# A trunk kernel whose S5 mixer changes between token order and chunk order: 64 ScalarE copies replaced by round trips through DRAM

## The chip, the cores and the metric

The kernel runs on one core of one Trainium2 chip. TensorE (PE; its weight loads are listed as PEld) multiplies, VectorE (DVE) and ScalarE (ACT) work elementwise, GpSimd (POOL) does a little arithmetic and issues some DMAs, and the sync engine (SP) issues the loads of the weights. The metric is the device time of one execution in microseconds (us), lower is better.

## The reference

A decoder trunk of two layers works on 256 tokens of width 1024. Each layer is a SwiGLU block, a token mixer, a second SwiGLU block (each followed by a layer norm) and a gate on an embedding. The mixer of the first layer has two halves, SSD and S5, on one input projection. Only S5 is touched:

```python
def s5_mixer(u, lam_re, ..., d_skip, w_glu, b_glu):      # u: (1, 256, 1024)
    ug = u.reshape(b, l, 64, 16)                          # 64 groups of 16 channels
    bu = jnp.einsum('blgp,gnp->blgn', ug, b_bar)          # complex states
    _, states = lax.associative_scan(linear_recurrence_combine, (a, bu), axis=1)
    y = jnp.real(jnp.einsum('blgn,gpn->blgp', states, c)) + d_skip * ug
    y = jax.nn.gelu(y.reshape(b, l, 1024))
    y = y * jax.nn.sigmoid(y @ w_glu + b_glu)
    return y
```

## The kernel before, in words

Weights come from DRAM in units of 1 MB (`wst`, two buffers, issued by SP). ACT casts each unit to a high part `wh` (line 61), DVE subtracts to get the low part `wl` (line 62), and every product is made of three matmuls. The kernel is one straight program for all engines; each engine works off its own instructions in order. That order is not written by hand: a scheduler sets it from estimated durations when the program is built, so a change of instructions also moves others.

The S5 mixer cuts the 256 tokens into 64 chunks of 4 steps. Its inputs u come as 1024 channels in two halves c = 0, 1 of 512. For each half, the projection is evicted from PSUM into `uT`, a tile of 128 channel partitions by 4 channel blocks by 256 tokens (lines 643 and 645; one of the two evictions of a half is on ACT, the other on DVE). In `U` a partition holds one step and one channel of a group of 32, and the free dimension holds 32 blocks of 64 chunks. So 32 partitions of `uT` with every fourth token go to another set of 32 partitions of `U`. Before, ACT does this by 16 copies of 32 partitions by 4 x 64 elements for each half (line 657). They read every fourth element.

The recurrence runs in 8 batches (`s5_batch`, called as recur(0) to recur(7)), of which 0 to 3 use the first half of U and 4 to 7 the second. A batch is a product with U on PE (`s5v`, line 678), a chain of rotation, scan and rotation on DVE (lines 686 to 694, result `S`), and a product back on PE (`s5y`, line 701), copied by ACT into `G` (line 703). Between the batches stand the projections of the SSD half (`bc`, `xs`, `z`). After four batches ACT applies the Gelu to `G` in place (line 709), and 16 ACT copies bring G back to channel partitions and token order in `yT` (line 719); they write every fourth element. `yT` is split into `yh` (ACT, line 722) and `yl` (DVE, line 723), the operands of the gate's product `glu` (lines 741 to 743). Tanh of it (`th`) times yT (line 746) is split again into `s5h` and `s5l` and goes to the output projection.

Batches are independent of the SSD half, whose heads (`seg`, `E`, `yp`, `cp`) run mostly behind the last batch.

Of the kernel before, what the change touches and what calls it, by code (L numbers as in the profile page):

```python
# [8 lines left out]
F32 = mybir.dt.float32  # L9
# [3 lines left out]
ALU = mybir.AluOpType  # L13
# [4 lines left out]
P = 128  # L18
D = 1024
NTOK = 256  # L20
# [13 lines left out]
def f32(ap):  # L34
    return ap.bitcast(F32)
# [49 lines left out]
def late(g, ins):  # L85

    g.tc.keep_in_program_order(ins)
# [10 lines left out]
def new_xT(g, name):  # L98
    return [g.xt.tile([P, KT, NTOK], F32R, tag=f"x{p}", name=f"x{p}_{name}") for p in "hl"]
# [532 lines left out]
    return e  # L632


def s5_inputs(g, pool, U, c):

    nc = g.nc
    uT = g.lnp.tile([P, 4, NTOK], F32, tag="ln_r", name=f"uT_{c}")

    def keep(h, ps):  # L640
        k = slice(2 * h, 2 * h + 2)
        if h:
            nc.vector.tensor_copy(uT[:, k, :], ps)
        else:
            nc.scalar.copy(uT[:, k, :], ps)

    if c:
        project_channels(g, f"u{c}", keep)
    else:
        channel_tiles(g, pool, f"u{c}", keep)  # L650
    Uv = U[:, 16 * c:16 * c + 16, :].rearrange("p (k q) c -> p k q c", q=4)
    uv = uT.rearrange("p k (c s) -> p k c s", s=4)
    for s in range(4):
        for q in range(4):
            dst = Uv[32 * s:32 * s + 32, :, q, :]
            src = uv[32 * q:32 * q + 32, :, :, s]
            nc.scalar.copy(dst, src)  # L657


def s5_batch(g, pool, U, G, b):  # L660
# [45 lines left out]
def s5_half_out(g, G, c, yh, yl):  # L706

    nc = g.nc
    op = nc.scalar.activation(G, G, AF.Gelu_apprx_tanh)
    if c:  # L710
        late(g, op)
    Gv = G.rearrange("p (k q) c -> p k q c", q=4)
    yT = g.lnp.tile([P, 4, NTOK], F32, tag="ln_r", name=f"yT_{c}")
    yv = yT.rearrange("p k (c s) -> p k c s", s=4)
    for q in range(4):
        for s in range(4):
            dst = yv[32 * q:32 * q + 32, :, :, s]
            src = Gv[32 * s:32 * s + 32, :, q, :]
            nc.scalar.copy(dst, src)  # L719
    for k in (0, 2):  # L720
        s, src = slice(4 * c + k, 4 * c + k + 2), yT[:, k:k + 2]
        nc.scalar.copy(yh[:, s], src)
        nc.vector.tensor_tensor(yl[:, s], src, f32(yh[:, s]), op=ALU.subtract)
    return yT


def s5_outputs(g, pool, yT, yh, yl):

    nc = g.nc
    hb = pool.tile([P, KT], F32, tag="hb", name="hb", bufs=1)  # L730
    nc.scalar.mul(hb, g.cols("bglu"), 0.5)
    sh = pool.tile([P, KT, NTOK], F32R, tag="sh", name="s5h", bufs=1)
    sl = pool.tile([P, KT, NTOK], F32R, tag="sl", name="s5l", bufs=1)
    for u in range(4):
        pieces = g.w.unit()
        for j in range(2):
            ct = 2 * u + j
            wh, wl = (p.rearrange("p (k c) -> p k c", k=KT) for p in pieces[j])
            ps = g.ps.tile([P, NTOK], F32, tag="acc", name=f"glu_{ct}", bufs=4)
            for k in range(KT):  # L740
                nc.tensor.matmul(ps, wh[:, k, :], yh[:, k, :], start=k == 0, stop=False)
                nc.tensor.matmul(ps, wh[:, k, :], yl[:, k, :], start=False, stop=False)
                nc.tensor.matmul(ps, wl[:, k, :], yh[:, k, :], start=False, stop=k == KT - 1)
            th = pool.tile([P, NTOK], F32, tag="th", name=f"th_{ct}", bufs=2)
            nc.scalar.activation(th, ps, AF.Tanh, scale=0.5, bias=hb[:, ct:ct + 1])
            nc.vector.scalar_tensor_tensor(th, th, 1.0, yT[ct // 4][:, ct % 4, :], op0=ALU.add, op1=ALU.mult)
            nc.scalar.mul(sh[:, ct, :], th, 0.5)
            nc.vector.scalar_tensor_tensor(sl[:, ct, :], th, 0.5, f32(sh[:, ct, :]), op0=ALU.mult, op1=ALU.subtract)
    return sh, sl


# [200 lines left out]
def ab_inputs(g, pool, s5pool, yh, yl):  # L952
# [37 lines left out]
    for c in range(2):  # L990
        s5_inputs(g, pool, U, c)
# [31 lines left out]
def channel_tiles(g, pool, name, out):  # L1023

    nc = g.nc
    ps = project(g, name, True)
    xb = []
    for t in range(NT):
        x = pool.tile([P, 512], F32, tag="ev", name=f"ev_{name}_{t}", bufs=2)
        nc.scalar.copy(x, ps[t])  # L1030
        xb.append(x)
    for h in range(2):
        tp = g.ps.tile([P, 2, NTOK], F32, tag="tr", name=f"ct_{name}_{h}", bufs=2)
        to_channels(g, xb, (2 * h, 2 * h + 1), tp)
        out(h, tp)
# [241 lines left out]
@with_exitstack  # L1277
def tile_trunk(ctx: ExitStack, tc: tile.TileContext, xnat, xTd, pT, lnr, colsd, cstd, abrow, abdt, s5bc, cdlr, cdgu,
               wall, out):
    nc = tc.nc  # L1280
    g = Ctx()
    g.nc, g.tc = nc, tc
    g.abrow, g.abdt, g.s5bc, g.cdlr, g.cdgu = abrow, abdt, s5bc, cdlr, cdgu
    g.const = ctx.enter_context(tc.tile_pool(name="const", bufs=1))
    g.wst = ctx.enter_context(tc.tile_pool(name="wst", bufs=2))
    g.wsp = ctx.enter_context(tc.tile_pool(name="wsp", bufs=6))
    g.xp = ctx.enter_context(tc.tile_pool(name="xp", bufs=1))
    g.xt = ctx.enter_context(tc.tile_pool(name="xt", bufs=1))
    g.lnp = ctx.enter_context(tc.tile_pool(name="lnp", bufs=2))
    g.small = ctx.enter_context(tc.tile_pool(name="small", bufs=2))  # L1290
    g.rows = ctx.enter_context(tc.tile_pool(name="rows", bufs=1))
    g.ps = ctx.enter_context(tc.tile_pool(name="ps", bufs=2, space=PSUM))
    g.dram = ctx.enter_context(tc.tile_pool(name="dram", bufs=1, space=DRAM))
    g.w = Weights(g, wall)
    g.lnr = lnr
    g.grow = {}

    nc.scalar.preload_act_table_set("silu_and_others")
    g.mhalf = g.const.tile([P, 1], F32, tag="mhalf", name="mhalf")
    nc.vector.memset(g.mhalf, -0.5)  # L1300
    g.s5dram = [g.dram.tile([P, PACK], F32, tag=f"s5d{b}", name=f"s5d{b}") for b in range(NB)]
    g.xT = new_xT(g, "in")
    for t in range(NT):
        xs = g.lnp.tile([P, KT, P], F32, tag="ln_r", name=f"xin_{t}")
        for h in range(2):
            s = slice(4 * h, 4 * h + 4)
            nc.scalar.dma_start(xs[:, s], xTd[t][:, s])
            split_xT(g, t, h, xs[:, s], g.xT)

    def load_constants():  # L1310
        cs = g.const.tile([P, cstd.shape[1]], F32, tag="cst", name="cs")
        nc.scalar.dma_start(cs, cstd)
        g.cst = lookup(cs, CST)
        g.ident = g.cst("ident")
        lc = g.const.tile([P, colsd.shape[1]], F32, tag="cols", name="lc")
        nc.scalar.dma_start(lc, colsd)
        g.cols = lookup(lc, COLS)

    def load_x():
        g.x = []  # L1320
        for t in range(NT):
            x = g.xp.tile([P, D], F32, tag=f"x{t}", name=f"x_in_{t}")
            late(g, nc.sync.dma_start(x, xnat[t * P:(t + 1) * P, :]))
            g.x.append(x)
        load_rows(g, 0, lnr)

    with tc.tile_pool(name="s5p", bufs=1) as s5p, tc.tile_pool(name="s5c", bufs=1) as s5c:
        g.s5p, g.s5c = s5p, s5c
        rest, half, loaded = [], [], []

        def first():
            load_constants()
            loaded.append(s5_load(g, 0))
            g.s5pe = s5c.tile([P, PACK_PE], F32, tag="s5pe", name="s5pe")
            nc.gpsimd.memset(g.s5pe[:, 1024:1536], 0.0)

        def params(b):
            if rest:
                rest.pop()()
            if b < NB:  # L1340
                if b % 4 == 0:
                    half[:] = [s5_half(g, b // 4, loaded[b // 4])]
                rest.append(s5_params(g, b, half[0]))
            if b == 3:
                loaded.append(s5_load(g, 1))

        hooks = {-1: first, 0: lambda: s5_scalars(g), NB + 2: load_x}
        for b in range(NB + 1):
            hooks[b + 1] = lambda b=b: params(b)
        ffn(g, "f00", 0, hooks)  # L1350
    mixer_ab(g, 1)
    load_rows(g, 2, lnr)
    with tc.tile_pool(name="pp0", bufs=1) as g.pp:
        ffn(g, "f01", 2)
        ple(g, 0, ple_proj(g, 0, pT), None)
    load_rows(g, 3, lnr)
    ffn(g, "f10", 3)
    load_rows(g, 4, lnr)
    mixer_cd(g, 4)
    load_rows(g, 5, lnr)  # L1360
    with tc.tile_pool(name="pp1", bufs=1) as g.pp:
        ffn(g, "f11", 5)
        ple(g, 1, ple_proj(g, 1, pT), out)
# [147 lines left out]
```

## Time and profile before

| | |
|---|---|
| time, median of 3 runs | 1270.6 us (1265.54, 1270.6, 1272.09) |
| the profiled execution's own time | 1264.66 us |
| its span | 1262.9 us |
| PE busy in it | 1210.2 us (96%) |
| DVE busy | 847.6 us (67%) |
| ACT busy | 660.9 us (52%) |
| POOL busy | 33.4 us (3%) |
| mean DMA rate | 188 GB/s |

The S5 mixer lies between about 225 and 445 us of the span. [...] A timeline row gives the start and the length of a run of equal instructions. "Idle" of PE costs time here; idle of the other engines does so only if PE waits for them.

### The profile page before, as it was taken

Reading aid. Unit: us, or ns where it says so; the run is one execution under the profiler, and the core shown is the slowest. Engines: PE = TensorE matmul, PEld = TensorE weight load, DVE = VectorE, ACT = ScalarE, POOL = GpSimd, SP = SyncE. Lnnn points to the kernel's source line nnn. Section 1 sums busy time; section 2 is a strip of 40 time slices with the busy share of each in tenths; the row PEclk is TensorE's granted clock in tenths of the full one; section 3 lists DMA queues with packets and bytes.
Section 4 is the critical chain, followed back from the end, with each engine's and each line's share of the span. In section 5 each row is a group of like instructions: output and inputs, shape, how many; then the busy total and the mean of one; then the engine's idle time right before and its main releaser. Section 6 shows DMA issues by size and latency. Waiting matters only on the chain.

```text
span 1262.9 us, 16242 instructions
## 1 busy us (share of the span) xinstructions
PE 1210.2 (96%) x6274; PEld 1020.0 (81%) x6274; DVE 847.6 (67%) x1353; ACT 660.9 (52%) x1008; POOL 33.4 (3%) x58
## 2 busy tenths in 40 slices
PE   6999999979896999999999999999999989999998
PEld 5888788779795987888888788888788877888886
DVE  6998774749685957645557655545779877555566
ACT  6566674584836653544444544444466635444434
POOL 0000000000000000000000000000100010000000
PEclk9999999989898999999999999999999999999999
DMA  7577767737551365655563655556443236555542
GB/s 272 202 250 249 264 249 280 265 128 256 179 193 41 119 208 172 211 199 178 189 224 110 233 191 180 196 184 215 157 164 134 100 109 218 196 187 200 173 160 100
DMA packets 39453, 237.93 MB, mean 188 GB/s; under 512 B 4528, under 2 KB 5200, under 8 KB 15696
## 3 DMA queue, kind: packets, MB, share of 16 engines
q1 hardware_dynamic: 30672, 206.06, 47.3%
q10 hardware_dynamic: 6096, 16.16, 3.8%
q0 software_dynamic: 2608, 14.68, 3.1%
q8 instruction: 49, 0.80, 0.3%
q14 instruction: 28, 0.23, 0.1%
HBM read 222.20 MB, written 14.68 MB: 188 GB/s over the span
## 4 chain that ended last, share of the span: by engine, by line
PE 86%; ACT 6%; DMA 3%; DVE 3%; issue 1%; ACTq 0%; POOL 0%; SPq 0%; DVEq 0%
PE gu_f L72 12%; PE gu_f L71 12%; PE gu_f L70 12%; PE acc_f L72 6%; PE acc_f L70 6%; PE acc_f L71 6%; DMA wst<-in_wall_dram 3%; ACT yT L719 2%; PE ht_f L209 1%; ACT U L657 1%; PE acc_ab L70 1%; PE acc_ab L71 1%; PE acc_ab L72 1%; DVE wl L62 1%; PE s5k L551 1%
## 5 line engine op out<-in xcount | busy, mean ns | idle before, releaser
L62 DVE TENSOR_TENSOR wl<-wst,wh 128x1024 fp32r<-128x1024 f32 (+1 forms) x378 | 453.4, 1215 | 281.0 <-ACT wh L61 275.0
L61 ACT CAST wh<-wst 128x1024 fp32r<-128x1024 f32 (+1 forms) x378 | 386.5, 1045 | 315.0 <-PE gu_f L72 104.1
L70 PE MATMUL acc_f<-wh,hh_f 128*128 128x512 f32 x352 | 137.5, 391 | 1.2 <-ACT hh_f L212 1.2
L71 PE MATMUL acc_f<-wl,hh_f 128*128 128x512 f32 x352 | 137.7, 391 | 0.0
L72 PE MATMUL acc_f<-wh,hl_f 128*128 128x512 f32 x352 | 136.4, 392 | 0.2 <-DVE hl_f L213 0.2
L70 PEld LDWEIGHTS acc_f<-wh,hh_f 128*128 128x128 f32 x352 | 66.1, 188 | 15.3 <-ACT hh_f L212 1.9
L72 PEld LDWEIGHTS acc_f<-wh,hl_f 128*128 128x128 f32 x352 | 66.1, 188 | 14.1 <-DVE hl_f L213 0.7
L71 PEld LDWEIGHTS acc_f<-wl,hh_f 128*128 128x128 f32 x352 | 66.1, 188 | 13.5
L70 PE MATMUL gu_f<-wh,xh_in 128*128 128x512 f32 x176 | 70.8, 407 | 6.1 <-ACT wh L61 6.1
L205 ACT ACTIVATE sg_f<-gu_f 128x256 f32<-128x256 f32 x88 | 33.6, 383 | 74.9 <-PE gu_f L72 73.1
L70 PE MATMUL gu_f<-wh,xh_ple 128*128 128x512 f32 x176 | 69.8, 396 | 1.8 <-ACT xh_ple L112 1.8
L71 PE MATMUL gu_f<-wl,xh_in 128*128 128x512 f32 x176 | 70.8, 404 | 0.0
L72 PE MATMUL gu_f<-wh,xl_in 128*128 128x512 f32 x176 | 70.6, 401 | 0.0
L70 PE MATMUL gu_f<-wh,xh_ab 128*128 128x512 f32 x176 | 69.8, 396 | 0.5 <-ACT xh_ab L112 0.5
L70 PE MATMUL gu_f<-wh,xh_cd 128*128 128x512 f32 x176 | 69.8, 396 | 0.3 <-ACT xh_cd L112 0.2
L72 PE MATMUL gu_f<-wh,xl_cd 128*128 128x512 f32 x176 | 69.1, 393 | 0.7 <-DVE xl_cd L113 0.7
L72 PE MATMUL gu_f<-wh,xl_ab 128*128 128x512 f32 x176 | 69.0, 392 | 0.7 <-DVE xl_ab L113 0.7
L71 PE MATMUL gu_f<-wl,xh_ab 128*128 128x512 f32 x176 | 68.8, 391 | 0.2 <-DVE wl L62 0.2
L72 PE MATMUL gu_f<-wh,xl_ple 128*128 128x512 f32 x176 | 68.8, 392 | 0.0
L71 PE MATMUL gu_f<-wl,xh_cd 128*128 128x512 f32 x176 | 68.7, 390 | 0.0
L71 PE MATMUL gu_f<-wl,xh_ple 128*128 128x512 f32 x176 | 68.7, 390 | 0.0
L206 DVE TENSOR_TENSOR sg_f<-sg_f,gu_f 128x256 f32<-128x256 f32 x88 | 36.5, 415 | 26.6 <-ACT sg_f L205 26.5
(467 smaller groups left out, 2443.1 us busy)
## 6 DMA issues: line engine op xcount, KB each, us to landing
wst<-in_wall_dram SPq DMA_DIRECT2D x185, 1024.0 KB, 4.9
s5d<-s5pk POOLq DMA_DIRECT2D x8, 896.0 KB, 4.8
s5d<-s5pe POOLq DMA_DIRECT2D x8, 768.0 KB, 3.7
row<-in_lnr_dram SPq DMA_DIRECT2D x12, 512.0 KB, 6.7
W<-s5d ACTq DMA_DIRECT2D x8, 512.0 KB, 3.9
Q<-s5d ACTq DMA_DIRECT2D x8, 512.0 KB, 5.8
tab<-s5d ACTq DMA_DIRECT2D x8, 384.0 KB, 3.8
wst<-in_wall_dram SPq DMA_DIRECT2D x4, 512.0 KB, 6.2
```

The lines of the kernel that those rows point to most:

```text
L61: ops = [nc.scalar.copy(wh[:, c], src[:, c])]
L62: ops.append(nc.vector.tensor_tensor(wl[:, c], src[:, c], f32(wh[:, c]), op=ALU.subtract))
L70: nc.tensor.matmul(out, xh, wh, start=first, stop=False)
L71: nc.tensor.matmul(out, xh, wl, start=False, stop=False)
L72: nc.tensor.matmul(out, xl, wh, start=False, stop=last)
L205: nc.scalar.activation(sg, ps[t][:, 0:256], AF.Silu)
L206: nc.vector.tensor_tensor(sg, sg, ps[t][:, 256:512], op=ALU.mult)
L209: nc.tensor.transpose(tp[:, k, :], sg[:, k * P:(k + 1) * P], g.ident)
L551: nc.tensor.matmul(kp[:, q, :], Eb[:, i, q, :], cv[:, i, hs.start + q, :], start=i == 0, stop=i == 1)
L657: nc.scalar.copy(dst, src)
L719: nc.scalar.copy(dst, src)
```

## The change

`uT` is now written step by step (all 64 chunks of step 0, then of step 1, and so on), so the evictions on lines 643 and 645 of before read their PSUM source with a stride of four elements. One DMA, issued by POOL, writes uT to a DRAM tile of 512 rows; four DMAs on the same queue, one for each step, read it back into 32 partitions of U each, in runs of 64 elements (256 bytes), 512 runs each. The outputs go the same way: one DMA writes G to DRAM, four read it into 32 partitions of yT each, again 512 runs of 256 bytes. yT, yh, yl, the gate's product and th now stand in step order. The product of line 746 reads th and yT in token order (every element 256 bytes from the last) and writes a new tile `gt` in token order, from which s5h and s5l are made.

```diff
+def by_step(ap):
+    return ap.rearrange("p k (s c) -> p k s c", s=4)
...
         if h:
-            nc.vector.tensor_copy(uT[:, k, :], ps)
+            nc.vector.tensor_copy(by_step(uT[:, k, :]), ps.rearrange("p k (c s) -> p k s c", s=4))
         else:
-            nc.scalar.copy(uT[:, k, :], ps)
+            nc.scalar.copy(by_step(uT[:, k, :]), ps.rearrange("p k (c s) -> p k s c", s=4))
...
-    Uv = U[:, 16 * c:16 * c + 16, :].rearrange("p (k q) c -> p k q c", q=4)
-    uv = uT.rearrange("p k (c s) -> p k c s", s=4)
-    for s in range(4):
-        for q in range(4):
-            dst = Uv[32 * s:32 * s + 32, :, q, :]
-            src = uv[32 * q:32 * q + 32, :, :, s]
-            nc.scalar.copy(dst, src)
+    d = g.perm[0][c]
+    nc.gpsimd.dma_start(d.rearrange("(p k) n -> p k n", k=4), uT)
+    dv = d.rearrange("(q r k) (s c) -> r k q s c", q=4, k=4, s=4)
+    for st in range(4):
+        to = U[32 * st:32 * st + 32, 16 * c:16 * c + 16, :].rearrange("p (k q) c -> p k q c", q=4)
+        nc.gpsimd.dma_start(to, dv[:, :, :, st, :])
...
-    Gv = G.rearrange("p (k q) c -> p k q c", q=4)
+    d = g.perm[1][c]
+    nc.gpsimd.dma_start(d.rearrange("(s r) (k q) c -> (s r) (k q) c", s=4, k=4), G)
+    dv = d.rearrange("(s r) (k q) c -> r q k s c", s=4, k=4)
     yT = g.lnp.tile([P, 4, NTOK], F32, tag="ln_r", name=f"yT_{c}")
-    yv = yT.rearrange("p k (c s) -> p k c s", s=4)
     for q in range(4):
-        for s in range(4):
-            dst = yv[32 * q:32 * q + 32, :, :, s]
-            src = Gv[32 * s:32 * s + 32, :, q, :]
-            nc.scalar.copy(dst, src)
+        nc.gpsimd.dma_start(by_step(yT[32 * q:32 * q + 32]), dv[:, q])
...
-            nc.vector.scalar_tensor_tensor(th, th, 1.0, yT[ct // 4][:, ct % 4, :], op0=ALU.add, op1=ALU.mult)
-            nc.scalar.mul(sh[:, ct, :], th, 0.5)
-            nc.vector.scalar_tensor_tensor(sl[:, ct, :], th, 0.5, f32(sh[:, ct, :]), op0=ALU.mult, op1=ALU.subtract)
+            gt = pool.tile([P, NTOK], F32, tag="gt", name=f"gt_{ct}", bufs=2)
+            by_token = lambda ap: ap.rearrange("p (s c) -> p c s", s=4)
+            nc.vector.scalar_tensor_tensor(gt.rearrange("p (c s) -> p c s", s=4), by_token(th[:, :]), 1.0,
+                                           by_token(yT[ct // 4][:, ct % 4, :]), op0=ALU.add, op1=ALU.mult)
+            nc.scalar.mul(sh[:, ct, :], gt, 0.5)
+            nc.vector.scalar_tensor_tensor(sl[:, ct, :], gt, 0.5, f32(sh[:, ct, :]), op0=ALU.mult, op1=ALU.subtract)
```

The scheduler moves other instructions with it. First ACT, where the inputs are brought to U, before (lines 657 and 645 are the copies into U and the eviction of the second half; the numbers in names are buffers):

```order
L645 COPY uT_2201<-ct_u_0_2276 128x512
L61 CAST wh_0_2665<-wst_2663 128x1024
L657 COPY U<-uT_2201 32x4x64 x16
L645 COPY uT_2304<-pc_u_0_2315 128x512
L61 CAST wh_1_2669<-wst_2663 128x1024
L61 CAST wh_0_2782<-wst_2780 128x1024
L61 CAST wh_1_2786<-wst_2780 128x1024
L657 COPY U<-uT_2304 32x4x64 x16
L605 COPY nout_dt<-nps_dt 32x256
```

and now (line 650 is the eviction):

```order
L650 COPY uT_2205<-ct_u_0_2280 128x512
L61 CAST wh_0_2647<-wst_2645 128x1024
L61 CAST wh_1_2651<-wst_2645 128x1024
L650 COPY uT_2297<-pc_u_0_2308 128x512
L61 CAST wh_0_2764<-wst_2762 128x1024
L61 CAST wh_1_2768<-wst_2762 128x1024
L61 CAST wh_0_2832<-wst_2830 128x1024
L605 COPY nout_dt<-nps_dt 32x256
```

The copies are gone, and the weight casts and `nout_dt` follow the evictions directly. On PE the first product with U (`s5v` of recur(0), line 678 before and 682 now) stood right behind the 16 small matmuls of `nps_dt`:

```order
L602 MATMUL nps_dt<-xh_f_2074,nws_dt 32x256
L602 MATMUL nps_dt<-xl_f_2075,nws_dt 32x256
L678 MATMUL s5v_2474<-U,W_2466 128x64 x8
L584 MATMUL pc_bc_0_2605<-xh_f_2074,wl_1_2602 128x256
L582 MATMUL pc_bc_0_2605<-xh_f_2074,wh_1_2601 128x256
```

and now comes after the first nine matmuls of the second unit of `bc`:

```order
L582 MATMUL pc_bc_1_2655<-xh_f_2078,wh_0_2647 128x256
L583 MATMUL pc_bc_1_2655<-xl_f_2079,wh_0_2647 128x256
L584 MATMUL pc_bc_1_2655<-xh_f_2078,wl_0_2648 128x256
L682 MATMUL s5v_2456<-U,W_2448 128x64 x8
L703 MATMUL s5y_2482<-U,T_2452 128x64
```

Between nps_dt and s5v there are now 28 matmuls of `pc_bc`, each 256 columns wide. Second, POOL's queue in this part of the program before (line 81 is a power that ends a norm's rsqrt):

```order
L81 TENSOR_TENSOR rs_r_ln_0_2110<-rs_w_ln_0_2108,mhalf 128x1
L81 TENSOR_TENSOR rs_r_ln_1_2165<-rs_w_ln_1_2163,mhalf 128x1
L81 TENSOR_TENSOR rs_r_ssd_3746<-rs_w_ssd_3744,mhalf 128x2
L81 TENSOR_TENSOR rs_r_ssd_3806<-rs_w_ssd_3804,mhalf 128x2
L81 TENSOR_TENSOR rs_r_ssd_3879<-rs_w_ssd_3877,mhalf 128x2
```

and now:

```order
L81 TENSOR_TENSOR rs_r_ln_1_2169<-rs_w_ln_1_2167,mhalf 128x1
L657 DMA udram_95<-uT_2205 128x1024
L661 DMA U<-udram_95 32x16x64 x4
L657 DMA udram_96<-uT_2297 128x1024
L661 DMA U<-udram_96 32x16x64 x4
L717 DMA ydram_97<-G_2447 128x1024
L721 DMA yT_2948<-ydram_97 32x16x64 x4
L717 DMA ydram_98<-G_3109 128x1024
L721 DMA yT_3641<-ydram_98 32x16x64 x4
L81 TENSOR_TENSOR rs_r_ssd_3706<-rs_w_ssd_3704,mhalf 128x2
```

Twenty DMAs stand between the powers of the layer norm and those of the SSD heads. Each group of four reads waits for the landing of the write ahead of it. Third, ACT behind the second Gelu (`E` are exponentials of the SSD heads, `yh` the split of yT), before:

```order
L709 ACTIVATE G_3138<-G_3138 128x1024
L719 COPY yT_3669<-G_3138 32x256 x16
L815 ACT_TABLE_LOAD
L815 ACTIVATE E_0_3699<-seg_0_3697 128x512
L815 ACTIVATE E_1_3708<-seg_1_3706 128x512
L868 ACTIVATE sq_0_3735,ss_3730<-y_0_3731 128x256
L722 CAST yh<-yT_3669 128x512 x2
L818 COPY end_3701<-E_0_3699 128x4
```

and now:

```order
L713 ACTIVATE G_3109<-G_3109 128x1024
L820 ACT_TABLE_LOAD
L820 ACTIVATE E_0_3659<-seg_0_3657 128x512
L823 COPY end_3661<-E_0_3659 128x4
L820 ACTIVATE E_1_3668<-seg_1_3666 128x512
L873 ACTIVATE sq_0_3695,ss_3690<-y_0_3691 128x256
L820 ACTIVATE E_0_3719<-seg_0_3717 128x512
L823 COPY end_3721<-E_0_3719 128x4
L820 ACTIVATE E_1_3728<-seg_1_3726 128x512
L724 CAST yh<-yT_3641 128x512 x2
```

The exponentials of the heads follow the Gelu directly, and the split of yT stands behind two heads' exponentials instead of one's.

## Rows read from the trace of the kernel before

**Rows 1.** The page: busy time by engine, and the chain that ended last by line.
```profile
PE 1210.2 (96%) x6274; PEld 1020.0 (81%) x6274; DVE 847.6 (67%) x1353; ACT 660.9 (52%) x1008; POOL 33.4 (3%) x58
...
PE gu_f L72 12%; PE gu_f L71 12%; PE gu_f L70 12%; PE acc_f L72 6%; PE acc_f L70 6%; PE acc_f L71 6%; DMA wst<-in_wall_dram 3%; ACT yT L719 2%; PE ht_f L209 1%; ACT U L657 1%; PE acc_ab L70 1%; PE acc_ab L71 1%; PE acc_ab L72 1%; DVE wl L62 1%; PE s5k L551 1%
```
**Rows 2.** PE's waits between 225 and 450 us (in total, times, longest).
```profile
PE cp L852 <- ACT E L815: 10.4, 1, 10.4
PE dt_ps L757 <- ACT nout_dt L605: 7.4, 1, 7.4
PE xs L976 <- ACT xsT L793: 4.3, 1, 4.3
```
**Rows 3.** Windows around them: PE, PEld, DVE, ACT, POOL busy, clock, DMA.
```profile
265.70:274.80 9.10, 0.42 (x3) 0.32 (x3) 3.07 (x6) 8.90 (x16) 0.00 (x0) 0.77 0.61 228
274.80:280.90 6.10, 6.10 (x28) 6.06 (x29) 5.07 (x10) 3.91 (x6) 0.00 (x0) 0.50 0.38 107
335.10:339.40 4.30, 0.00 (x0) 0.00 (x1) 1.45 (x3) 4.22 (x7) 0.00 (x0) 0.94 0.33 91
339.40:349.20 9.80, 9.80 (x46) 9.71 (x47) 8.14 (x12) 6.52 (x10) 0.00 (x0) 0.50 0.59 195
396.50:406.90 10.40, 0.04 (x1) 0.00 (x0) 0.85 (x2) 10.22 (x17) 0.00 (x0) 0.69 0.00 1
406.90:410.60 3.70, 3.68 (x11) 3.13 (x12) 3.11 (x7) 2.09 (x6) 0.00 (x0) 0.50 0.02 4
```
**Rows 4.** ACT's timeline there: start, length, what.
```profile
249.87 10.55 ACT L657 COPY U<-uT 32x256 f32<-32x256 f32 x16
...
263.91 9.14 ACT L657 COPY U<-uT 32x256 f32<-32x256 f32 x14
...
274.37 0.36 ACT L605 COPY nout_dt<-nps_dt 32x256 f32<-32x256 f32 x1
...
326.33 9.84 ACT L719 COPY yT<-G 32x256 f32<-32x256 f32 x15
...
394.53 10.43 ACT L719 COPY yT<-G 32x256 f32<-32x256 f32 x16
404.98 1.28 ACT L815 ACT_TABLE_LOAD   x1
```
**Rows 5.** The copies into U as a group: count, busy us, mean ns.
```profile
L657 ACT COPY U<-uT 32x256 f32<-32x256 f32 x32 | 20.6, 644 | 0.4
```
**Rows 6.** Windows with PE's pace, and with both PE and DVE full.
```profile
245.00:250.00 5.00, 5.00 (x44) 5.00 (x43) 2.96 (x4) 3.28 (x5) 0.00 (x0) 1.00 0.78 233
285.00:330.00 45.00, 45.00 (x361) 43.77 (x361) 43.20 (x93) 23.09 (x33) 0.00 (x0) 1.00 0.75 262
410.00:440.00 30.00, 30.00 (x219) 27.29 (x218) 29.06 (x66) 19.03 (x43) 2.18 (x3) 0.99 0.33 108
```
**Rows 7.** POOL's s5pe writes (768 KB each): issue in ns, landing min/median/max.
```profile
L559 POOL DMA_DIRECT2D s5d<-s5pe x8: 531/531/533, 89.1 to 220.2; - x8
...
DMA to landing us min/median/max: 3.5/3.7/7.6
```
**Rows 8.** POOL's reads of pt (256 KB each), landing.
```profile
DMA to landing us min/median/max: 3.0/3.5/3.9
```
**Rows 9.** DMA queues of SP and ACT: packets, MB, share of 16 engines.
```profile
q1 hardware_dynamic: 30672, 206.06, 47.3%
q10 hardware_dynamic: 6096, 16.16, 3.8%
```
**Rows 10.** When uT of the first half is done, and when s5v began.
```profile
246.94 0.68 DVE L643 COPY uT<-ct_u 128x512 f32<-128x512 f32 x1
...
259.52 0.78 PE L678 MATMUL s5v<-U,W 128*128 128x64 f32 x6
```
**Rows 11.** Strided DVE operands elsewhere: two lines, ns min/median/max over strides.
```profile
L1115 DVE TENSOR_TENSOR X_g<-X_g,gqk x7: 411/418/423, 931.3 to 983.1; 128x256 f32<-128x256 f32 x7
...
L1141 DVE COPY_PREDICATED at_g<-cs,lv_g x12: 427/448/795, 947.3 to 989.0; 127x256 f32<-127x256 int32 x2, 126x256 f32<-126x256 int32 x2, 124x256 f32<-124x256 int32 x2, 120x256 f32<-120x256 int32 x2
```

More of the change, by code (lines that the diff above doesn't have):

```diff
@@ L1301, in tile_trunk @@
     g.s5dram = [g.dram.tile([P, PACK], F32, tag=f"s5d{b}", name=f"s5d{b}") for b in range(NB)]
+    g.perm = [[g.dram.tile([512, NTOK], F32, tag=f"u{c}", name=f"udram{c}") for c in range(2)],
+              [g.dram.tile([P, 16, 64], F32, tag=f"y{c}", name=f"ydram{c}") for c in range(2)]]
     g.xT = new_xT(g, "in")
```

## The prediction

> **What bounds the kernel now.** I read the page first, for the engines' shares and the chain [rows 1]: PE is busy for 96% of the span, and yet the chain runs through ACT's copies into yT (2%) and U (1%), some 38 us. So PE is the bound almost everywhere, and the copies can matter only where PE stands still. Second, PE's waits around the S5 mixer [rows 2]: three long ones, each ended by an ACT instruction that stood behind copies. Third, windows around them [rows 3], to see what else was idle and which clock PE then got. Fourth, ACT's timeline [rows 4], to see that the engine holding PE up really was in the copies.
>
> Three places come out of it, which I call U, Y0 and Y1. At U, nout_dt ends PE's wait at 274.4, behind 9.1 + 1.3 us of copies into U; the wait is 7.4 us, and with 1.3 us more in the same window PE is idle for 8.7 (0.42 busy of 9.10). At Y0, PE waits 4.3 us for an SSD activation queued behind the first 16 copies into yT. At Y1 it waits 10.4 us for an exponential that stands behind the second 16. [...] So PE loses 8.7 + 3.05 = 11.8 at U, 4.3 + 4.9 = 9.2 at Y0, 10.4 + 1.85 = 12.2 at Y1: 33.2 us, the most that the change can give back.
>
> **What it removes.** 64 ACT copies at 0.644 us [rows 5], 41 us of ACT. What of it lies beside PE's work is worth nothing; what lies on the path is the 33.2. Two other limits come next. DVE at U: it is idle for 6.0 + 1.0 us in the two windows there [rows 3], and in the 45 us that follow it is 96% busy while PE is at 100% [rows 6], so DVE's chains of the recurrence will make PE wait again here and there: I leave 3.0 of the 11.8 and count 8.8. At Y0 DVE has over 4 us idle in the two windows, and the order puts no new wait ahead of PE's work: I leave 1.0 for a partly cold clock and count 8.2. At Y1 the SSD heads that now follow the Gelu directly need 23 DVE instructions by the new order; DVE does 66 in 29.06 of the 30 us there [rows 6], 0.44 us each, so they take 10.1 us, and PE has about half as much to do beside them. I leave 4.5 idle and 1.3 of clock and table load.
>
> **What it adds: four round trips through DRAM.** The trace has no transfer in 256-byte runs, so I put the trip T, from the tile being ready to its copy having landed, together from neighbours. The write of 512 KB is like POOL's s5pe writes of 768 KB [rows 7]: landed 3.7 us after issue (3.5 to 7.6). Then POOL issues four reads. An issue takes 0.53 us there for 128 rows; these have 512 runs each, so between 0.53 and 2.1 us each, 2.1 to 8.5 for four. I take 2.1, the row itself, though none shows an issue of more runs. The last read lands like pt's [rows 8], 3.5 us (3.0 to 3.9, or 7.6 as the worst of the writes). And the packets: 2048 of 256 bytes for a half, 128 on each of 16 engines. SP's queue takes 47.3% of 16 x 1262.9 us for 30672 packets of 6.7 KB, 312 ns each; ACT's 126 ns for packets of 2.65 KB [rows 9]. A line through both gives about 5 ns + 46 ns per KB, thus 17 ns at 256 bytes, 2.1 us for 128; the upper end is the ACT queue's whole 126 ns, 16 us. I take the line, as its two points lie almost on proportionality. T = 3.7 + 2.1 + 3.5 + 2.1 = 11.4 us; the ends are 8.1 and nearly 40.
>
> **What waits for a trip.** U: uT is complete at 246.94 + 0.68 = 247.6 [rows 10], plus up to 0.6 for evictions that now read every fourth element (ACT's strided copies pay 0.644 against 0.36 for the same count [rows 4, 5]). s5v began at 259.5 and now has 28 more matmuls of 5.00 / 44 = 0.114 us [rows 6] ahead, so it needs U at 262.7: 14.5 us of cover. If it is late, everything behind it in PE's order is late. The second half has 40 us more. Y0: after the Gelu ended at 326.3, PE ran on until 335.1 without ACT; the new order adds the fifth batch's products and some SSD transposes before DVE's yl, which stands inside the chain of recur(5), holds that chain: some 27 small matmuls, about 3 us at PE's pace, so about 12 us of cover; behind yh on ACT stand weight casts, behind yl on DVE the rest of the chain, and PE waits for both. Y1: PE's gate matmuls on the second half stand behind the 10.1 us of heads' work, which starts 1.9 us after the Gelu (table load and one exponential); yh and yl take 1.8 us of that: 10.2 us of cover. POOL's powers for the SSD heads are queued behind the last reads, but their operands come from later DVE work. So lateness costs (T - 14.5) + (T - 12) + (T - 10.2), each term only where positive: at T = 11.4 it is 1.2, all at Y1.
>
> The strided product gt: eight instructions, in a stretch where DVE is full, so any extra shows. The nearest row is a two-operand product over strides of one to 64 elements, 411 to 423 ns throughout; a predicated copy on short runs goes from 0.45 to 0.80 us [rows 11]. I take 0; the upper end is 8 x 0.35 = 2.8 us, and a gain is excluded, since the number of elements is the same and 411 ns is the least of any stride.
> [...]
> [...]
>
> **The sum.** 8.8 + 8.2 + (12.2 - 4.5 - 1.3 - 1.2 = 5.2) = 22.2 us. The profiled execution took 1264.66 us (its span 1262.9), so 1242.5; it lies 5.9 us below the median of the three runs, so 1248.4, and I say 1248. Its own range is 1240 to 1258 (T from 8 to 15, gt up to 2.8, DVE's share off by 3).
>
> **Rivals.**
> Slower, by slow small packets: if a 256-byte packet costs what ACT's mean packet does, T = 3.7 + 2.1 + 3.5 + 16.1 = 25.4 and lateness is 39.5 us, 38.3 more than counted, so the 22.2 turn into a loss of 16.1: 1280.8, or 1287 by the median. It decides from T = 20.0, or 84 ns a packet. For it: no packet so small and strided is in the trace, and they compete with the weight stream, at 0.75 of the DMA engines in 285 to 330 [rows 6]. Against: the two queues' times scale with size. Chance 0.13.
> Trips late, by the issues: if POOL's issue grows with the number of runs, T = 17.8, lateness is 16.7 and 6.7 us of gain are left: 1264 by the median. For it: an issue here has four times the runs of any in the trace; against, the equal 531 ns [rows 7]. Chance 0.17; part of it falls within no change.
> Everything comes back: if DVE keeps up and T is short, 33.2 us, 1237. For it: ACT also casts weights earlier, so DVE can begin sooner; against, 96% of DVE behind U. Chance 0.10.
> The forecast keeps 0.60. That the copies stay is excluded by the order.
>
> **How the numbers follow.** About 0.5%, 6.4 us, is what a measurement of this kernel can tell from no change, so faster is below 1264 and slower above 1277. Faster: 0.60 + 0.10 + 0.05 of the late trips = 0.75; same 0.12; slower 0.13. The range is 1235 to 1270: it leaves out most of the slow case and the lowest tail.
>
> **What would show it.** In the changed profile: ACT busy lower by about 40 us; PE's wait at dt_ps gone and s5v not waiting for a DMA; yT's reads landing about 11 us after each Gelu; glu waiting at most 1 us for yh; the clock at 1.00 through 266 to 281. Reads that land over 20 us after the write's issue, POOL issues of 2 us, or s5v waiting for U would prove me wrong, and DVE at 100% with PE idle behind U would mean that I left too little for DVE.

## The result, and the profile after

The changed kernel took 1237.2 us (median of 4 runs, 1235.1 to 1237.9) beside 1269.9 us for the kernel before: a ratio of 0.9745, 95% interval 0.9725 to 0.9765. With the runs beside the experiments, before has 27 runs (median 1268.35, 1263.6 to 1272.1) and the changed kernel 8 (median 1237.2, 1235.1 to 1238.7), so the gain is 31.1 us. From one profiled execution to the other it is 28.0 us (1264.66 to 1236.71). The forecast was 1248; the time lies inside the range given, but outside the 1240 to 1258 of the forecast case, and on the number of the rival "everything comes back" (1237).

The page of the changed kernel, to be read beside [rows 1]: engines (busy us, share of the span, instructions), the DMA packets, and POOL's queue (packets, MB, share of 16 engines).

```profile
PE 1202.8 (97%) x6274; PEld 1011.3 (82%) x6274; DVE 848.5 (69%) x1353; ACT 621.1 (50%) x944; POOL 48.5 (4%) x78
...
DMA packets 40797, 242.12 MB, mean 196 GB/s; under 512 B 4848, under 2 KB 5520, under 8 KB 17040
...
q0 software_dynamic: 3952, 18.88, 4.3%
```

ACT lost 64 instructions and 39.8 us. PE's waits between 225 and 450 us, where [rows 2] had 10.4, 7.4 and 4.3 us:

```profile
PE tp_ln L142 <- DVE x_ln L138: 2.3, 2, 1.9
PE pj_u L70 <- ACT xh_f L112: 0.9, 1, 0.9
PE sc L809 <- ACT E L820: 0.8, 2, 0.6
PE glu L743 <- ACT yh L724: 0.8, 1, 0.8
PE seg L818 <- DVE cr L859: 0.5, 1, 0.5
```

The three waits are gone, and none has taken their place; the longest left (1.9) is that of a layer norm ahead of the mixer. The windows at the three places answer to [rows 3]. A window row has the stretch and its length, the busy time of PE, PEld, DVE, ACT and POOL, the share of TensorE's full clock that was granted (0.50 is half clock), the DMA share and GB/s:

```profile
265.00:275.00 10.00, 10.00 (x85) 9.84 (x83) 9.83 (x22) 4.79 (x8) 0.00 (x0) 1.00 0.77 231
275.00:305.00 30.00, 30.00 (x261) 30.00 (x261) 29.87 (x67) 12.75 (x19) 0.00 (x0) 1.00 0.80 271
325.00:340.00 15.00, 15.00 (x131) 15.00 (x131) 13.94 (x24) 5.74 (x9) 0.00 (x0) 1.00 0.81 289
370.00:385.00 15.00, 12.70 (x65) 8.64 (x64) 13.38 (x31) 8.99 (x19) 3.48 (x5) 1.00 0.22 72
385.00:390.00 5.00, 5.00 (x29) 3.69 (x30) 5.00 (x13) 1.88 (x6) 1.36 (x1) 1.00 0.00 0
```

PE is full and the clock at 1.00 behind U and Y0. DVE is full behind U too (29.87 of 30), and still PE does not wait for it. Only at Y1, between 370 and 385, is PE idle for 2.3 us, and the clock stays up. The trips in POOL's timeline (start, length, idle before and what ended it):

```profile
248.63 0.59 POOL L657 DMA_DIRECT2D udram<-uT  x1 [14.70 <-ACT uT L650]
253.04 2.95 POOL L661 DMA_DIRECT2D U<-udram  x4 [3.82 <-DMA udram<-uT]
...
374.06 0.57 POOL L717 DMA_DIRECT2D ydram<-G  x1 [51.35 <-ACT G L713]
378.43 2.90 POOL L721 DMA_DIRECT2D yT<-ydram  x4 [3.80 <-DMA ydram<-G]
```

The second trip of y ends when ACT starts yh, 1.07 us late by its timeline:

```profile
383.54 1.14 ACT L724 CAST yh<-yT 128x512 fp32r<-128x512 f32 x2 [1.07 <-DMA yT<-ydram]
```

That is 9.5 us after the write's issue. At U the reads land 5.2 us (median) after their issue, about 260.5, and s5v starts at 263.2, not waiting for them.

**One account for all runs.** I cut every trace into windows of 1 us and summed two losses of PE: idle (1 minus its busy time) and half clock (busy time x (1 minus the granted clock)). By stretch of the span, in us, idle + half clock; "rest" is everything outside 245 to 470; a cell with one number is idle alone:

| kernel | U: 245 to 305 | Y0: 305 to 365 | Y1: 365 to 470 | rest | span |
|---|---|---|---|---|---|
| before | 8.9 + 3.1 | 4.3 + 4.9 | 10.9 + 1.8 | 27.7 + 3.2 | 1262.9 |
| before, second profile | 8.7 + 2.6 | 4.3 + 6.3 | 10.9 + 2.7 | 28.7 + 9.1 | 1269.8 |
| changed | 0 | 0 | 3.6 | 27.5 + 3.2 | 1234.9 |
| changed, second profile | 0 | 0 | 3.6 | 27.8 + 6.3 | 1236.5 |
| inputs alone | 0 | 5.4 + 4.1 | 9.3 + 1.7 | 28.1 + 4.9 | 1251.0 |
| outputs alone | 8.7 + 2.5 | 0 | 2.1 | 28.0 + 6.6 | 1246.2 |
| copies in step order | 1.4 | 1.1 | 8.1 + 1.9 | 26.8 + 9.0 | 1246.7 |
| product in step order | 0 | 0 | 3.6 | 28.0 + 3.4 | 1234.1 |
| u, two copies more | 0.2 | 0 | 5.1 | 26.0 + 7.7 | 1238.5 |
| y, one copy more | 0 | 0 | 4.3 | 26.2 + 8.9 | 1238.9 |
| all trips, three copies more | 0 | 2.7 + 1.9 | 8.2 + 6.6 | 27.3 + 7.3 | 1253.0 |
| DVE +10.9 us | 0.3 | 4.3 + 3.0 | 4.9 + 3.6 | 28.3 + 4.9 | 1248.8 |
| DVE +5.4 us | 0 | 0 | 4.7 | 26.0 + 8.6 | 1238.4 |
| tile to tile | 0 | 0 | 7.2 + 3.3 | 27.8 + 8.9 | 1246.7 |

The span minus these losses is 1196 to 1201 us in every row: PE's work at full clock. So what parts the rows is nearly all in the losses. The three places cost 33.9 us before and 3.6 after.

The last stretch ends at 470 us in every row, whatever the kernel is doing there. In the changed kernel 1.3 of the 3.6 us are short waits at the first products of the next block (`gu_f`, from 455 us), which in the kernel before start at 485 and count as "rest". The mixer itself keeps 2.3 us, the idle time of the window from 370 to 385 above. In the runs with inputs alone, with all trips longer and with DVE +10.9, those waits lie mostly or wholly behind 470, so against the changed kernel these rows lose about 1 us more than the table's difference.

### The profile page after: what moved, and what is told of

Read it like the earlier page. It is cut to its first block, busy times and chain, and to the rows that moved or that the text cites. A ratio compares the mean times of both kernels' runs of the same rounds, so it can differ in the third digit from the quotient of the medians.

```text
span 1234.9 us, 16234 instructions
## 1 busy us (share of the span) xinstructions
PE 1202.8 (97%) x6274; PEld 1011.3 (82%) x6274; DVE 848.5 (69%) x1353; ACT 621.1 (50%) x944; POOL 48.5 (4%) x78
## 4 chain that ended last, share of the span: by engine, by line
PE 72%; issue 5%; DVE 3%; DMA 1%; POOL 0%; ACT 0%; DVEq 0%; ACTq 0%; POOLq 0%
PE gu_f L72 10%; PE gu_f L71 10%; PE gu_f L70 9%; PE acc_f L72 5%; PE acc_f L70 5%; PE acc_f L71 5%; PE acc_ple L71 1%; PE acc_ab L70 1%; PE acc_ab L72 1%; PE acc_ab L71 1%; PE acc_ple L72 1%; PE acc_ple L70 1%; PE ht_f L209 1%; PE lv_h L1140 1%; PE lv_g L1140 1%
## 5 line engine op out<-in xcount | busy, mean ns | idle before, releaser
L71 PEld LDWEIGHTS acc_f<-wl,hh_f 128*128 128x128 f32 x352 | 66.1, 188 | 13.5
```

The costliest lines, as they stand in the source:

```text
L71: nc.tensor.matmul(out, xh, wl, start=False, stop=False)
```

## Experiments

Every edit starts from the changed kernel unless said. Times beside 1237.2 (changed) and 1268.35 (before).

**1. Inputs alone, outputs alone.** The functions of the other half are those of before.

> Only the inputs go by way of DRAM; the outputs are copied by ACT and the gate's product is as before. Theory, ACT's copies block PE at three places that add up: the loss at U (11.8 us of idle and half clock in the trace before) goes, Y0 and Y1 stay, so 11.8 us are gained: about 1258 us beside 1269.9, ratio 0.991; PE's wait at dt_ps gone, its waits at xs (4.3) and cp (10.4) still there. The prediction's own term, with DVE as the next limit behind U, says 8.8 us: 1261. Rival, the gain comes from ACT's 40 us being free anywhere (earlier weight casts): half the copies, half the gain, 16 us: 1254.

Measured: 1252.7 us (1250.7 to 1253.4), ratio 0.9873 (0.9855 to 0.9892). Its two longest waits of PE:

```profile
PE cp L856 <- ACT E L819: 9.3, 1, 9.3
PE xs L980 <- ACT xsT L797: 5.4, 1, 5.4
```

> Only the outputs go by way of DRAM, with the strided gate product; the inputs are copied by ACT as before. Theory of three places: Y0 (9.2 us) and Y1 (12.2 us) go but for 3 us of idle that the changed kernel still shows at Y1 and 1.6 us of gt, so 16.8 us are gained: about 1253 us, ratio 0.987; the wait at dt_ps (7.4) stays, with half clock behind it. The prediction's own terms say 13.4 us: 1256.5. Rival, half the copies, half the gain: 1254, not to be told apart here by the time alone but by dt_ps. If this and the run with the inputs alone add up to the whole change, the places are independent.

Measured: 1247.2 us (1246.3 to 1250.4), ratio 0.9837 (0.9817 to 0.9858). Its longest wait:

```profile
PE dt_ps L763 <- ACT nout_dt L605: 7.5, 1, 7.5
```

By the medians the gains are 15.6 and 21.1 us, more than the theory's 11.8 and 16.8, and the first fits the rival's 16. By the traces each half removes its own places and leaves the others: from the first profile of before, spans are 11.9 and 16.7 us shorter, 28.6 together for the 28.0 of the whole. The medians together give 36.7, more than the 31.1 of the whole change; what each has on top of its trace is, in the main, the distance of the runs of before from their first profile (1268.35 - 1264.66 = 3.7 us), taken up in experiment 3. The rival, a gain spread over the span, falls: with the inputs alone Y0 and Y1 lose 20.5 us where they lost 21.9, and the rest loses 33.0 where it lost 30.9.

**2. The copies kept, but between tiles in step order; the product's stride taken away.**

```diff
-    d = g.perm[0][c]   # and its five DMAs
+    for s in range(4):
+        for q in range(4):
+            nc.scalar.copy(Uv[32 * s:32 * s + 32, :, q, :], by_step(uT)[32 * q:32 * q + 32, :, s, :])
...
+            nc.scalar.copy(by_step(yT)[32 * q:32 * q + 32, :, s, :], Gv[32 * s:32 * s + 32, :, q, :])
```

> The 64 ACT copies stay, but between tiles that are both in step order (runs of 64 elements on either side), no trip through DRAM; evictions and gate product as in the changed kernel. Theory, the length of ACT's block is what PE pays: with 0.36 us a copy (nout_dt's time for 32 x 256) a block of 16 shrinks from 10.3 to 5.8 us, so 4.5 us less at U, 4.3 (all of its idle) and its clock loss of 4.9 at Y0, 4.5 at Y1, minus 1.6 for gt: 16.6 us gained, about 1253. Rival, a copy's time is not in the stride: blocks stay 10.3 us and the time is that of before plus gt, 1271.

Measured: 1247.3 us (1244.6 to 1248.6), ratio 0.9831 (0.9810 to 0.9851). The copies into U (ns min/median/max) against the 644 of [rows 5], the first block of 16 against the 10.55 us of [rows 4], and PE's longest wait:

```profile
L660 ACT COPY U<-uT x32: 399/403/406, 251.9 to 268.2; 32x256 f32<-32x256 f32 x32
...
251.88 6.67 ACT L660 COPY U<-uT 32x256 f32<-32x256 f32 x16
...
PE cp L857 <- ACT E L820: 6.6, 1, 6.6
```

A block of 16 falls to about 6.5 us (16 x 0.403), not to 5.8, so each block is 3.9 us shorter. That nearly clears U (1.4 us left), where two blocks stand ahead of nout_dt, while I had counted one; it nearly clears Y0 (1.1 left), where one block had 4.3 us of idle behind it. At both the clock no longer falls; I had left U its clock loss. Y1 keeps 10.0. Two thirds of the gain (21.0 of 31.1 us) need no DMA at all, only copies without the stride. Nor do they need the new order of PE's work around the batches: in this trace every batch's s5v stands behind as many other matmuls as before (1241 for the first, against 1269 in the changed kernel). How much of the last third comes from the new order was not tested.

> The changed kernel, but the gate's product reads and writes contiguously, so that its result stays in step order: the return to token order is left out. Theory, eight products of 0.62 us become 0.42, and DVE is not full where seven of them stand: between nothing and 1.6 us less, 1235.5 to 1237.2. Rival, the prediction's zero for the stride (product rows at 0.41 whatever the stride): the product's time does not move. If DVE's chain set the end there, all 1.6 us would show.

Measured: 1238.7 us (1235.8 to 1239.4). The product in this run, and in the changed kernel:

```profile
L749 DVE SCALAR_TENSOR_TENSOR gt<-th,yT x8: 409/414/419, 392.3 to 412.1; 128x256 f32<-128x256 f32 x8
```
```profile
L750 DVE SCALAR_TENSOR_TENSOR gt<-th,yT x8: 601/618/631, 392.8 to 412.9; 128x256 f32<-128x256 f32 x8
```

The stride costs 0.20 us an instruction, 1.6 in all, and none of it shows in the time: the account is 3.6 us at Y1 in both.

**3. Before and changed a second time.**

> The kernel before, unchanged, for a second profile: its nine other runs took 1266.0 to 1271.5 us at mean clocks of 0.983 to 0.976, the first profile 1264.66 at 0.984. [...]

Measured: 1271.6 us, clock 0.977, close to the upper end of its runs. The same three waits:

```profile
PE cp L852 <- ACT E L815: 10.4, 1, 10.4
PE dt_ps L757 <- ACT nout_dt L605: 7.5, 1, 7.5
PE xs L976 <- ACT xsT L793: 4.3, 1, 4.3
```

Windows behind two of them and at a place far behind the mixer:

```profile
340.00:355.00 15.00, 13.49 (x66) 13.40 (x67) 11.38 (x19) 8.22 (x13) 0.00 (x0) 0.54 0.64 235
...
1016.00:1024.00 8.00, 6.58 (x33) 6.58 (x34) 5.56 (x9) 1.58 (x3) 2.63 (x3) 0.57 0.28 113
...
411.00:416.00 5.00, 5.00 (x18) 3.70 (x17) 4.76 (x10) 1.99 (x6) 0.00 (x0) 0.54 0.01 3
```

Idle is 52.5 us in total against 51.9, half clock 20.7 against 13.0: this 7.7 us makes up the 6.9 us of span. So these two runs of one kernel differ by how much half clock they catch, not by waits; the mean clocks of its other runs (0.986 at 1263.6 us, 0.976 at 1271.5) point the same way. My theory put all of it behind the three waits; the rival was longer waits, or a loss elsewhere in the span. Only 1.8 of the 7.7 lies at the three places; 5.9 lies away from the change, as at 1016 to 1024, where the first profile had 1.00.

> The changed kernel, unchanged, as the neighbour of the three runs beside it and for a second profile. The theory of the three places: no wait of PE above 2.5 us between 240 and 450 us and the clock at 1.00 there again; a time of 1235 to 1240, with what differs from the first profile (1236.71) lying in half-clock stretches away from the S5 mixer. Rival, the first profile was a lucky one and one of the three places shows idle or half clock again.

Measured: 1237.3 us (1235.9 to 1238.7), ratio 0.9772 (0.9747 to 0.9796) to the seven runs of before beside it. Idle at Y1 is again 3.6 us, nothing at U and Y0; the difference to the first profile is 3.1 us of half clock in the rest. As expected.

**4. Longer trips.** In each trip d is copied to one, two or three further DRAM tiles before it is read:

```diff
+    for hop in g.hop_u[c]:
+        nc.gpsimd.dma_start(hop, d)
+        d = hop
```

> The changed kernel with two more DRAM to DRAM copies in each trip of u, so about 9 us more (two issues of 0.6 and two landings of 3.6 to 4): U lands near 270 us instead of 261. The new order puts 107 more matmuls ahead of the first s5v. The prediction's cover of 14.5 us from uT to s5v, with everything behind it late: about 6 us slower, 1243. Rival, the order has other work for PE, and DVE's chains have room later: within 1.5 us of 1237. Third, DVE's chains are the limit from U to the second Gelu: all 9 us show at Y1, 1246.

Measured: 1239.5 us (1238.0 to 1240.3). The first U is read back from here, 16.3 us after the write's issue (250.37) instead of 4.4:

```profile
266.64 2.96 POOL L664 DMA_DIRECT2D U<-hopu  x4 [1.79 <-issue]
```

A trip is then some 24 us, 9.5 beyond the cover of 14.5 that I had worked out, yet U shows 0.2 us and Y1 1.5 more than without. The order was made anew with s5v behind 107 more matmuls, and the recurrence made up for most of its late start: the first Gelu begins 19.8 us later than in the changed kernel, the second 3.2. The rival is the nearest: 2.3 us by the medians and 1.7 at the three places, where it allowed 1.5 and the theory had 6.

> The changed kernel with one more DRAM to DRAM copy in each trip of y, about 4.5 us more; PE's order around it is nearly the same. The trace of the changed kernel shows PE waiting 0.8 us for yh at Y1, so there the cover is used up: 3.5 to 4.5 us slower, nearly all at the first gate product behind the second Gelu, 1241 to 1242, and nothing at Y0. The prediction's cover of 10.2 us says the same in size. Rival, PE has SSD products to do there anyway: below 1 us.

Measured: 1240.6 us (1239.8 to 1242.3). The median, 3.4 above the changed kernel, fits the theory's 3.5 to 4.5, but its trace does not: PE waits for yh nowhere, idle at Y1 is 4.3 against 3.6, and the span's other 3.3 us are less than the 5.7 us that half clock grew by in the rest. The mechanism I expected is not in the trace; the time alone would have confirmed it. Nor is the order the same at Y1: four of the heads' `seg` products now stand ahead of the gate's first product on the second half, which begins at 391.6 us instead of 384.2. The rival, below 1 us, is the better reading, though the two can't be parted by this run's time.

> The changed kernel with three more DRAM to DRAM copies in every trip of u and y: trips of about 25 us, as in the prediction's slower rival. By the prediction's formula the lateness is (25 - 14.5) + (25 - 12) + (25 - 10.2) = 38 us: 1275. Theory after the runs with longer trips (two copies in u cost 2.3 us, one in y 3.4): the order is made anew and puts other work in front, so far less shows; what can't be filled is the end, Y1, where the trip of the second half has only the SSD heads and the first half's gate products beside it: 8 to 14 us with the clock, 1245 to 1251. If it stays under 1242, a trip of 25 us is hidden everywhere.

Measured: 1254.6 us (1253.6 to 1257.0), 17.2 above the changed kernel beside it and still below before: ratio 0.9911 (0.9886 to 0.9935). The trips are 21 to some 30 us long (the second of y: write issued at 385.1, yh on its landing at 405.8; the first of u: from 250.3, reads issued until 276.9). That is less than half of the formula's 38, and more than my 8 to 14. PE now stands at half clock behind both halves of y:

```profile
359.00:374.00 15.00, 12.75 (x63) 12.26 (x63) 10.01 (x20) 1.41 (x3) 2.38 (x4) 0.54 0.40 124
404.00:412.00 8.00, 6.67 (x33) 6.28 (x34) 5.52 (x17) 3.27 (x9) 1.10 (x2) 0.57 0.50 154
```

Of the 15.8 us that the three places lose more, 8.5 are half clock.

**5. More work for DVE.**

```diff
         nc.vector.tensor_tensor(s, src, bc(sinT, 1, 2), op=mul)
+        if b < 4:      # b < 2 in the second run
+            nc.vector.tensor_tensor(c, src, bc(cosT, 1, 2), op=mul)
+            nc.vector.tensor_tensor(s, src, bc(sinT, 1, 2), op=mul)
```

> The changed kernel, but in batches 0 to 3 DVE computes the two products of each rotation twice: 16 more instructions of 0.68 us, 10.9 us of DVE between 265 and 340 us, where it is at 100% for 35 us while PE never waits. The prediction left 3.0 us because DVE would be the next limit there: with no room at all, the 10.9 us show, 1248. Rival, 100% busy hides work done ahead of need (weight splits), with room behind: the windows of 305 to 345 us show some 5 us of DVE idle, so at most 6 us and likely under 3 show: 1237 to 1240.

Measured: 1250.7 us (1250.3 to 1253.7), 13.5 more for 10.9 us of DVE. After 354.4 us PE stands still for 4.1 us while DVE works, and the half clock follows. The trace does not say what ended this wait; PE goes on at 358.5, 0.1 us after DVE's instruction `rots`.

```profile
355.00:358.00 3.00, 0.00 (x0) 0.00 (x0) 3.00 (x5) 0.00 (x0) 0.00 (x0) 1.00 0.99 224
358.00:369.00 11.00, 10.36 (x48) 10.20 (x49) 6.14 (x13) 1.51 (x3) 0.00 (x0) 0.53 0.53 190
```

The three places lose 12.5 us more: 5.9 idle and 6.6 half clock. Neither theory had counted the second part.

> As the run with DVE's rotations computed twice, but in batches 0 and 1 alone: 8 more instructions of 0.68 us, 5.4 us of DVE between 265 and 305. There 10.9 us more of DVE cost 13.5 us. Theory, DVE has some 5 us of room (10.9 added, 5.9 more idle of PE in that profile, and the rest half clock behind the idle): at most 1.5 us slower, 1237 to 1239. Rival, no room, each us of DVE shows: 5.4 us and more with the clock, 1243 or above.

Measured: 1240.1 us (1236.7 to 1240.2), 2.7 more than the changed kernel beside it; the three places lose 1.1 more, the rest is half clock elsewhere. So some 5 us of DVE fit in before PE waits for them. Where they went is seen in DVE's busy time (its column is the third after the length) between 305 and 345 us, in the changed kernel and in this run:

```profile
305.00:345.00 40.00, 40.00 (x297) 37.83 (x296) 34.10 (x61) 21.54 (x30) 3.48 (x5) 1.00 0.77 265
```
```profile
305.00:345.00 40.00, 40.00 (x299) 37.90 (x299) 37.11 (x74) 18.95 (x26) 3.47 (x5) 1.00 0.80 276
```

DVE was full only up to 305; behind that it had 5.9 us idle, of which 3.0 are used here. But the order is another one too, in this run and in the one with four batches: 62 more matmuls of other products stand ahead of the third batch's s5v and 125 ahead of the fourth's. How much of the room is DVE's own and how much the new order made was not parted.

**6. Tile to tile.**

```diff
-    nc.gpsimd.dma_start(d.rearrange("(p k) n -> p k n", k=4), uT)   # and the four reads
+            nc.gpsimd.dma_start(Uv[32 * s:32 * s + 32, :, q, :], uv[32 * q:32 * q + 32, :, s, :])   # 16 for each half
...   # the outputs likewise
```

> The 64 copies become 64 DMAs from tile to tile on POOL's queue, in runs of 256 bytes, without the stop in DRAM; evictions and gate product as in the changed kernel. A trip is then 16 issues of 0.53 us (the row for 128 runs) and one landing of 3.5 to 5: 12 to 13.5 us beside some 12 now. Theory, only ACT's blocks mattered: 1236 to 1240, no difference. Rival, the issue on POOL is the trip: if an issue takes 0.84 us as the reads of the changed kernel do, a trip is 17 to 18.5 us and the first s5v or the gate waits, 1240 to 1246. Second rival, the stop in DRAM costs: 3 us faster.

Measured: 1246.2 us (1243.4 to 1248.7), 8.9 slower than the changed kernel beside it.

```profile
L721 POOL DMA_DIRECT2D yT<-G x32: 548/548/551, 328.9 to 384.7; - x32
...
DMA to landing us min/median/max: 1.7/3.7/6.8
```

An issue takes 0.548 us, so 16 take 8.7 and a trip about 12.4, as the theory said, and yet the time is at the upper end of the rival's. 6.9 us of it is at Y1 (7.2 + 3.3 against 3.6), though ACT waits only 0.3 us for these transfers; the second Gelu ended already 2.6 us later. The rest is half clock elsewhere. The order is another here as well: the first batch's s5v stands behind 22 more matmuls of other products than in the changed kernel, the fourth's behind 96 more. Whether that order or the transfers made the recurrence later stays open.

## Why the prediction was right, and where it was off

**What bounds the kernel, and the 33.2 us.** Right, and the step that carries the sign. Its 3.05, 4.9 and 1.85 us of clock loss are half of PE's busy time in the three windows of [rows 3] in which 0.50 of the clock was granted (6.10, 9.80 and 3.68 us); the account has 3.1, 4.9 and 1.8. With the idle time it gives 12.0, 9.2 and 12.7 us at U, Y0 and Y1 before; each half of the change clears its own. That the time came out on the number of the rival that everything comes back, 1237, is in part luck. What it asked for did hold: DVE keeps up and the trip is short. But it took 33.2 us from a median that was 2.2 us high, and the gain was 31.1.

**The leftovers: the step that failed.** I left 3.0, 1.0 and 7.0 us behind (11.0); by the account 3.6 are left, all in the stretch Y1, so 7.4 us more came back. At U the reason given was DVE's 96% [rows 6]. DVE is indeed full there, and PE is never idle beside it: a full DVE was not PE's next limit. Experiment 5 shows room for some 5 us more of DVE's work, in an order made for it. That DVE's time there holds work done ahead of need, such as its 9.5 us of weight splits between 265 and 305, is argued and not shown. At Y0 PE was never idle and the clock stayed at 1.00, so the 1.0 for a cold clock was not needed. At Y1 the mixer's own idle time is 2.3 us, for which I had 4.5 of heads and 1.2 of lateness: the heads held PE up for 1.5 of it, and the lateness is there as the 0.8 that glu waits for yh. The 1.3 for clock and table load did not show, since the clock stayed at 1.00.

**From the profile to the median.** The second part that failed: I carried the 5.9 us by which the three runs lay above the profile over to the changed kernel. Its runs lie 0.5 above its profile. The three runs of before were high (1270.6; 27 runs give 1268.35), and what the two profiles of a kernel differ by is half clock (7.7 us in those of before, 3.1 in those of the changed kernel), not a constant. Leftovers, this, and 2.5 us that PE's own work took longer at full clock (1198.1 to 1200.6, whose cause stays open) make up most of the miss of 1248.4 - 1237.2 = 11.2: 7.4 + 5.4 - 2.5 = 10.3. The account has 33.9 at the three places where I had 33.2, which is 0.7 more, and the rest is rounding.

**The trip.** T = 11.4 was about right as a sum (9.5 us from the write's issue at Y1, about 12 at U), not in its terms; that these came out together near 11.4 is luck. The lower end of 8.1 does not come out of the rows either (3.5 + 2.1 + 3.0 is 8.6 before any packet), but nothing rested on it. The four issues took 2.9 us, not 2.1 (each 0.71 to 0.96 for 512 runs, overlapping a little, against 0.53 for 128 rows), far below the 8.5 of the late-by-issues rival. The packets were not of 256 bytes: the page has 1344 more of them on POOL's queue and 320 more under 512 B, and 4.19 MB more. 320 is 16 for each of the 20 DMAs; the 1024 others average 4.1 KB, for the writes and the reads together. By that mean a packet held some 16 runs of 256 bytes, so the term of 17 ns x 128 had no object. What runs of 256 bytes cost by themselves no run here tests: the reads landed 5.2 us after issue at U and 3.3 at the outputs (medians), where [rows 8] had 3.5.

**The cover and the break-even.** Wrong in size: I held the order fixed and let every us beyond 14.5, 12 and 10.2 show, break-even at T = 20.0. A program whose trips take 21 to 30 us is still faster than before. In every run with longer trips the order was made for them and put other work in front of their readers, so less of the lateness showed than the formula has, about 17 us of 38. This does not give the price of the slower rival, in which packets would have been slow under the order as it stood: no run here has late trips in the changed kernel's own order. What speaks against that rival is the packets themselves.

**gt and the evictions.** gt: taken 0, measured 0.20 x 8 = 1.6 us (0.618 against 0.414 each), of which the account shows nothing. I had misread my row, the product at 0.41 [rows 11]: line 1115 of before takes runs of 1 to 64 neighbouring elements with gaps as long, so every second element at the least, and never one element in 64. The evictions: up to 0.6 expected, none measured:

```profile
L650 ACT COPY uT<-ct_u 128x512 f32<-128x512 f32 x1 | 0.6, 580 | 0.0
```

It took 577 ns before; DVE's of the same half took 683 in both.

**What would show it.** ACT 39.8 us lower, dt_ps's wait gone, s5v not waiting for a DMA, glu waiting 0.8 us for yh, the clock at 1.00 behind U: all seen. yT landed about 10 us after the Gelu instead of 11.

## What to carry to other kernels

Where an in-order engine does a block of small copies between a producer and PE, price the block by PE's wait and by the half clock that follows it in the profile: together they were the whole effect here (33.9 us before, 3.6 after, for 28.0 between the profiles), and the engine's own busy time (39.8 us less on ACT) was not. A neighbouring engine at 100% is not yet the next limit (DVE was busy for 29.87 of 30 us here, PE for all 30), and an added latency that the scheduler knows of costs what the new order can't fill (17.2 us here), not what the old order's cover leaves of it (38): both are found by adding a known amount of work or delay, and by looking at what the order then became. Before moving data by DMA, try the same copies without their stride; here that brought two thirds of the gain (21.0 of 31.1 us).

## What the runs showed of the hardware

- ACT's copy of 32 x 256 f32 in SBUF took 0.644 us with one side at every fourth element (before) and 0.403 us with runs of 64 (copies in step order). From PSUM, 128 x 512 read at every fourth element took ACT 0.580 us and DVE 0.683 (changed), and contiguous 0.577 and 0.683 (before). DVE's product in SBUF took 0.618 us with both inputs read at every 64th element (changed), and 0.414 contiguous (product in step order).
- POOL's DMA issue took 0.53 us for 128 rows (before), 0.548 for a tile-to-tile DMA of 128 runs (tile to tile), and 0.71 to 0.96 for 512 runs of 256 bytes (changed).
- The same wait was followed by half clock of different length: behind the 4.3 us at Y0 PE lost 4.9 us to half clock in one profile of before and 6.3 in the other.
